# Half of the modulation-vector chunks beside the delta rule go to TensorE

## The chip, the core and the metric

The kernel runs on one core of a Trainium2 chip. The metric is the device time of one execution in microseconds. Three executions of the kernel before took 2535.95, 2541.6 and 2545.97 us, so the median is 2541.6 us. The engines are named as in the profile: PE is the matrix engine, PEld its weight loads, DVE the vector engine, ACT the scalar engine, POOL the GpSimd engine, SP the engine that issues most DMAs.

## What is computed

The reference is a two-layer trunk over 256 latent tokens of width 2048, in float32. Cut to what matters:

```python
for layer in range(2):
    mx = split(silu(c) @ w_ada[layer] + b_ada[layer], 6)       # six modulation vectors of 2048
    h_x = rms_norm(x, g_pre_mix) * (1 + mx[1]) + mx[0]
    if layer == 0:   # attention heads, and a bidirectional gated delta rule, side by side
        y_x = attention_deltanet_mixer(h_x, h_c, ...)          # h_c: the context, modulated alike
    else:
        y_x = fourier_mix(h_x) @ w_fourier
    x = x + mx[2] * rms_norm(y_x, g_post_mix)
    f_x = swiglu(rms_norm(x, g_pre_ffn) * (1 + mx[4]) + mx[3], w_gate, w_up, w_down)
    x = x + mx[5] * rms_norm(f_x, g_post_ffn)
```

The change concerns the product `silu(c) @ w_ada`. Each modulation vector is a matrix of 2048 x 2048 against one vector.

## The kernel before

The first two modulation vectors of layer 0 are made at the start (`ada_half`, lines 359 to 383), where each 128 x 1024 piece of the matrix goes to DVE, to GpSimd or to PE by a letter in the string `WHO`. A piece on PE is eight matmuls of one 128 x 128 block each against a column of `c2c`, the silu of the vector as columns, into one PSUM tile, and one ACT copy out of it.

The other ten vectors are background work. They are cut into 160 chunks of 128 output elements, 16 to a vector, and each chunk into two halves, so 320 units. A unit (`ada_units`, line 277) loads a 128 x 1024 piece of 512 KB into one of the two buffers named `araw` (line 285) and multiplies and sums it on DVE against the vector spread over all partitions (`cb`), in one instruction with an accumulator (`ada_dot`, line 274). `bg(n)` (line 298) runs n units. `every(us)` sets a pace: `step()`, which is called between the matmuls of the projections, runs one unit each time that `clock` has moved on by that many microseconds. `clock` is no time of the chip: `mm` (line 132) adds to it, for each matmul, its columns over 2400, times four for plain float32 operands, with at least 64 columns counted. `ada_until(m)` runs what is missing of the first m vectors.

The weights of all projections come through `load_w1` (line 183): a 512 KB load into one of three buffers named `raw` (in some stretches two loads of five take `araw`), ACT rounds each half of it to fp32r (`whi`, line 197), and DVE or POOL subtracts to get the rest (`wlo`, line 203). Each product takes three fp32r matmuls.

Beside the delta rule the pace is 4.3 and all `wlo` are POOL's. The delta rule of the four groups of heads is written as generators (`gdn_a`, `gdn_b`, `fin_k` and others) that `step()` advances between the matmuls of the remaining projections. The order on each engine is set when the program is built, by a list scheduler that may move an instruction ahead of the place where it was written when its inputs and its buffer are free; each engine then runs its list strictly in order. In the two feed-forward parts the order of DVE is the written one.

Two masks of triangles (`k_tri`, 128 x 2 x 128) are read twice: at the start, and again at line 490 for the running sums of the gates, each time into one of three buffers named `K1` by a DMA on POOL's queue.

## Time and profile before

| | us |
|---|---|
| three executions, median | 2541.6 |
| the profiled execution, as timed | 2532.5 |
| its span, first to last instruction | 2530.7 |
| PE busy in the span | 2361.0 |
| DVE busy | 1836.5 |
| ACT busy | 1304.6 |
| POOL busy | 423.4 |

The profile is of one execution. Busy time of an engine is the time in which one of its instructions was running; for PE the end of a matmul is modelled, and matmuls overlap. Stages in the trace: up to 191 us the first two modulation vectors with the first projection; from 191 to about 720 us the delta rule, attention and their projections; to about 806 us the output projection; then the feed-forward part of layer 0 to about 1590, the Fourier mix to about 1790, and the feed-forward part of layer 1. A row of waits counts the idle time of an engine before an instruction by what ended it.

### The profile page before, as it was taken

How to read it: one execution, taken by the hardware profiler on the slowest of the kernel's cores; microseconds unless marked ns; L12 is line 12 of the kernel's file. 1: busy time of each engine (PE TensorE's matmuls, PEld its weight loads, DVE VectorE, ACT ScalarE, POOL GpSimd, SP SyncE). 2: the span in 40 equal slices, each digit the busy share in tenths (PEclk: the TensorE clock that was granted, in tenths of full speed). 3: DMA queues.
4: the chain of work that ended last, by engine and by line, in shares of the span. 5: the costliest groups of instructions: out<-in, count | busy, mean ns of one | idle time of the engine just before them, and what ended most of it. 6: DMA issues, size and time to landing. Idle time of an engine off the chain costs nothing.

```text
span 2530.7 us, 39215 instructions
## 1 busy us (share of the span) xinstructions
PE 2361.0 (93%) x14232; PEld 1992.5 (79%) x14232; DVE 1836.5 (73%) x3232; ACT 1304.6 (52%) x2385; POOL 423.4 (17%) x331
## 2 busy tenths in 40 slices
PE   5888978888899999999999999899999999999997
PEld 5877868877677788888888887697788888888886
DVE  7998778778757677877778778847666665555556
ACT  4446533535375655454445554746654554445455
POOL 4873523335531100000000000101100000000001
PEclk8889989989999999999999999999999999999998
DMA  7665778678846668989998988626577777666665
GB/s 274 229 234 179 241 217 261 232 231 263 278 158 210 207 212 316 315 314 312 320 318 308 319 312 316 237 95 214 192 236 242 229 240 233 192 191 186 194 202 199
DMA packets 218530, 611.14 MB, mean 241 GB/s; under 512 B 68920, under 2 KB 69928, under 8 KB 217568
## 3 DMA queue, kind: packets, MB, share of 16 engines
q1 hardware_dynamic: 168016, 581.59, 68.6%
q10 hardware_dynamic: 46528, 15.21, 2.7%
q0 software_dynamic: 3792, 11.85, 1.4%
q8 instruction: 111, 1.82, 0.3%
q14 instruction: 83, 0.68, 0.1%
HBM read 595.16 MB, written 13.40 MB: 240 GB/s over the span
## 4 chain that ended last, share of the span: by engine, by line
PE 71%; DVE 12%; DMA 7%; issue 4%; ACT 2%; POOL 2%; SPq 0%; ACTq 0%; DVEq 0%; POOLq 0%
PE acc L132 65%; PE sm L132 5%; DMA araw<-in_ada_d 4%; DVE araw L274 3%; DVE E L274 1%; DVE wlo L203 1%; POOL C L359 1%; DMA T<-dy 1%; PE sm L1237 1%; DVE C L514 1%; DVE T L730 1%; DMA T<-dz 1%; DMA S<-in_ctx 1%; DVE S L1154 1%; ACT whi L197 1%
## 5 line engine op out<-in xcount | busy, mean ns | idle before, releaser
L197 ACT ACTIVATE whi<-raw 128x512 fp32r<-128x512 f32 (+1 forms) x1306 | 817.7, 630 | 858.2 <-DVE wlo L203 457.3
L203 DVE TENSOR_TENSOR wlo<-raw,whi 128x512 fp32r<-128x512 f32 x1140 | 796.6, 707 | 442.9 <-ACT whi L197 440.4
L132 PE MATMUL acc<-whi,S 128*128 128x512 f32 x3312 | 1043.0, 393 | 3.9 <-ACT whi L197 2.2
L132 PEld LDWEIGHTS acc<-whi,S 128*128 128x128 f32 x3312 | 624.7, 189 | 134.3 <-ACT whi L197 3.1
L132 PE MATMUL acc<-wlo,S 128*128 128x512 f32 x1656 | 649.0, 392 | 2.9 <-POOL wlo L203 1.7
L274 DVE SCALAR_TENSOR_TENSOR araw<-araw,cb 128x1024 f32<-128x1024 f32 x320 | 411.9, 1288 | 67.0 <-DMA araw<-in_ada_d 66.3
L132 PEld LDWEIGHTS acc<-wlo,S 128*128 128x128 f32 x1656 | 312.9, 189 | 67.6 <-POOL wlo L203 2.7
L203 POOL TENSOR_TENSOR wlo<-raw,whi 128x512 fp32r<-128x512 f32 x166 | 240.6, 1462 | 431.5 <-ACT whi L197 416.2
L132 PE MATMUL acc<-S,whi 128*128 128x256 f32 x1152 | 246.4, 306 | 22.5 <-ACT whi L197 9.4
L132 PEld LDWEIGHTS acc<-S,whi 128*128 128x128 f32 x1152 | 201.6, 209 | 25.3 <-ACT whi L197 10.5
L1114 POOL DMA_DIRECT2D drow<-K x4 | 2.0, 508 | 1274.8 <-DVE K L1112 1274.8
L132 PE MATMUL acc<-S,wlo 128*128 128x256 f32 x576 | 173.8, 303 | 9.9 <-DVE wlo L203 6.8
L132 PEld LDWEIGHTS acc<-S,wlo 128*128 128x128 f32 x576 | 121.0, 210 | 12.5 <-DVE wlo L203 8.7
L132 PE MATMUL acc<-whi,ZT 128*128 128x512 f32 x384 | 122.5, 393 | 0.0
L132 PE MATMUL acc<-whi,KCH 128*128 128x512 f32 x320 | 110.9, 403 | 1.1 <-ACT whi L197 1.1
L132 PE MATMUL acc<-whi,A 128*128 128x512 f32 x312 | 106.0, 395 | 0.0
L132 PE MATMUL acc<-whi,T 128*128 128x512 f32 x296 | 99.7, 393 | 0.0
L132 PEld LDWEIGHTS acc<-whi,ZT 128*128 128x128 f32 x384 | 72.1, 188 | 15.5
L132 PE MATMUL acc<-wlo,KCH 128*128 128x512 f32 x192 | 77.8, 405 | 4.3 <-DVE wlo L203 4.1
L132 PE MATMUL acc<-wlo,ZT 128*128 128x512 f32 x192 | 74.8, 390 | 0.0
L132 PEld LDWEIGHTS acc<-whi,KCH 128*128 128x128 f32 x320 | 62.2, 194 | 15.3 <-ACT whi L197 1.5
L132 PE MATMUL acc<-wlo,T 128*128 128x512 f32 x176 | 68.6, 390 | 0.0
(447 smaller groups left out, 2945.1 us busy)
## 6 DMA issues: line engine op xcount, KB each, us to landing
raw<-in_w_gu SPq DMA_DIRECT2D x347, 512.0 KB, 4.4
araw<-in_ada_d SPq DMA_DIRECT2D x320, 512.0 KB, 4.7
raw<-in_w_dn SPq DMA_DIRECT2D x179, 512.0 KB, 4.4
raw<-in_w_att SPq DMA_DIRECT2D x40, 512.0 KB, 4.5
raw<-in_w_gdn SPq DMA_DIRECT2D x34, 512.0 KB, 4.4
raw<-in_w_out SPq DMA_DIRECT2D x30, 512.0 KB, 3.5
ZT<-in_ada_s SPq DMA_DIRECT2D x24, 512.0 KB, 3.6
raw<-in_w_four SPq DMA_DIRECT2D x21, 512.0 KB, 3.5
```

What stands on the lines that cost most here:

```text
L132: nc.tensor.matmul(out, l, r, start=start, stop=stop)
L197: S.activation(hi[:, :w], raw[:, c:c + w], AF.Copy)
L203: eng.tensor_sub(lo[:, :w], raw[:, c:c + w], hi[:, :w].bitcast(F32))
L274: V.scalar_tensor_tensor(out=junk, in0=w, scalar=1.0, in1=rows, op0=ALU.mult, op1=ALU.mult, accum_out=dst)
L359: nc.gpsimd.tensor_tensor(out=pr, in0=raw[:, ql], in1=ccb[h][:, ql], op=ALU.mult)
L514: V.scalar_tensor_tensor(out=ca[:, :, lo:hi], in0=pv[:, :, lo + o:hi + o], scalar=wconv[:, blk, j:j + 1], in1=ca[:, :, lo:hi], op0=ALU.mul ...
L730: V.tensor_tensor(out=tv, in0=Zi[:, 0:k, k:k + 1].to_broadcast([P, k, 16 - k]), in1=Y[:, k:k + 1, k:16].to_broadcast([P, k, 16 - k]), op=A ...
L1114: nc.gpsimd.dma_start(drow.rearrange("h k p -> (h k) p"), gt)
L1154: V.scalar_tensor_tensor(out=x[:, t, sl], in0=y[:, t, sl], scalar=r, in1=x[:, t, sl], op0=ALU.mult, op1=ALU.add)
L1237: nc.tensor.transpose(p[:, i * P:(i + 1) * P], hv[t][:, i * P:(i + 1) * P], ident)
```

## The change

`NPE = 60` and `by_pe(n)`: of the first 60 chunks each odd one, so 30 chunks or 60 units, all in the first four background vectors, is computed on PE as eight matmuls against `c2c` and an ACT copy of one column into the accumulator tile. The host lays those pieces out as 128 x 128 blocks that PE can take as stationary operands. The load of a unit is a function of its own, `ada_load(i)`, and `bg` calls it for the unit it is about to run and for the one after; `ada_until` leaves out the last one ahead. `raw` has four buffers in place of three. `k_tri` gets a buffer of its own and is read once. The region of on-chip memory that holds descriptors of DMAs from GpSimd is set to 8192 bytes per partition.

```diff
--- before.py
+++ after.py
@@ -63,9 +63,15 @@
 XE = 3
 RING0 = 'oAakzrraoz'
 RING = 'rozza'
+NPE = 60
 SK_EV = 2
 SK_M = 1
 SK_P = 2
+
+
+def by_pe(n):
+
+    return n < NPE and n % 2 == 1
 
 
 @with_exitstack
@@ -183,7 +189,7 @@
     def load_w1(src, n=1024, keep=()):
 
         nload[0] += 1
-        raw = T([P, 1024], "araw", 2) if pace[1] and not pace[0] and nload[0] % 5 > 2 else T([P, 1024], "raw", 3)
+        raw = T([P, 1024], "araw", 2) if pace[1] and not pace[0] and nload[0] % 5 > 2 else T([P, 1024], "raw", 4)
         nc.sync.dma_start(raw[:, :n], src)
         out = []
         for c in range(0, n, 512):
@@ -217,7 +223,7 @@
     nc.gpsimd.memset(ones, 1.0)
     epsc = C([P, 1], "epsc")
     nc.gpsimd.memset(epsc, EPS)
-    tri = T([P, 2, P], "K1", 3)
+    tri = C([P, 2, P], "tri")
     nc.gpsimd.dma_start(tri, a["k_tri"])
 
     maskd = []
@@ -274,33 +280,48 @@
         V.scalar_tensor_tensor(out=junk, in0=w, scalar=1.0, in1=rows, op0=ALU.mult,
                                op1=ALU.mult, accum_out=dst)
 
+    plan = [(l, m, k, h) for l in range(2) for m in range(2 if l == 0 else 0, 6) for k in range(KC) for h in range(2)]
+    ada_raw = {}
+    ada_n = [0]
+
+    def ada_load(i):
+        if i < len(plan) and i not in ada_raw:
+            ada_raw[i] = T([P, 1024], "araw", 2)
+            nc.sync.dma_start(ada_raw[i], a["ada_d"][i // 2, i % 2])
+
     def ada_units():
-        n = 0
-        for l in range(2):
-            for m in range(2 if l == 0 else 0, 6):
+
+        for i, (l, m, k, h) in enumerate(plan):
+            ada_load(i)
+            raw = ada_raw.pop(i)
+            if k == h == 0:
                 ac = T([P, KC, 2], "adaacc", 2)
-                for k in range(KC):
-                    for h in range(2):
-                        raw = T([P, 1024], "araw", 2)
-                        nc.sync.dma_start(raw, a["ada_d"][n, h])
-                        ada_dot(raw, cb[:, h], ac[:, k, h:h + 1], raw)
-                        if k == KC - 1 and h == 1:
-                            V.tensor_reduce(out=mc[:, l, m], in_=ac, op=ALU.add, axis=AX.X)
-                            V.tensor_tensor(out=mc[:, l, m], in0=mc[:, l, m], in1=bada[:, l, m], op=ALU.add)
-                        yield
-                    n += 1
+            if not by_pe(i // 2):
+                ada_dot(raw, cb[:, h], ac[:, k, h:h + 1], raw)
+            else:
+                p = sm()
+                for kk in range(8):
+                    mm(p[:, 0:1], raw[:, kk * P:(kk + 1) * P], c2c[:, h * 8 + kk, 0:1], kk == 0, kk == 7)
+                S.activation(ac[:, k, h:h + 1], p[:, 0:1], AF.Copy)
+            if k == KC - 1 and h == 1:
+                V.tensor_reduce(out=mc[:, l, m], in_=ac, op=ALU.add, axis=AX.X)
+                V.tensor_tensor(out=mc[:, l, m], in0=mc[:, l, m], in1=bada[:, l, m], op=ALU.add)
+            yield
 
     ada_it = ada_units()
-    ada_n = [0]
-
-    def bg(n):
-        for _ in range(n):
-            if ada_n[0] < 320:
+
+    def bg(n, more=True):
+
+        for q in range(n):
+            if ada_n[0] < len(plan):
+                ada_load(ada_n[0])
+                if more or q < n - 1:
+                    ada_load(ada_n[0] + 1)
                 next(ada_it)
                 ada_n[0] += 1
 
     def ada_until(mods):
-        bg(max(0, 32 * mods - ada_n[0]))
+        bg(max(0, 32 * mods - ada_n[0]), False)
 
     def rstd(ssq, n, dim):
         r = col(n)
@@ -339,7 +360,7 @@
     def ada_half(i):
 
         k, m, h = i // 4, i // 2 % 2, i % 2
-        tag, n = {"a": ("araw", 2), "o": ("OG", 2), "z": ("ZT", 4), "r": ("raw", 3), "k": ("KCH", 2), "4": ("T4", 2), "A": ("A", 2)}[RING0[nraw[0]] if nraw[0] < len(RING0) else RING[nraw[0] % len(RING)]]
+        tag, n = {"a": ("araw", 2), "o": ("OG", 2), "z": ("ZT", 4), "r": ("raw", 4), "k": ("KCH", 2), "4": ("T4", 2), "A": ("A", 2)}[RING0[nraw[0]] if nraw[0] < len(RING0) else RING[nraw[0] % len(RING)]]
         nraw[0] += 1
         raw = T([P, 1024], tag, n)
         nc.sync.dma_start(raw, a["ada_s"][i])
@@ -487,8 +508,6 @@
     lbmg = C([P, 4, 8, 2], "lbmg")
     egc = C([P, 4, 8, 2], "egc")
     egl = C([P, 4, 8, 2], "egl")
-    tri = T([P, 2, P], "K1", 3)
-    nc.gpsimd.dma_start(tri, a["k_tri"])
     pgc = sm()
     for d in range(2):
         gd = T([P, 32], "gd", 2)
@@ -1468,7 +1487,9 @@
     for l in range(2):
         for m in range(2 if l == 0 else 0, 6):
             for k in range(KC):
-                dl.append(wa[l, :, m, k, :].T.reshape(P, 2, 1024).transpose(1, 0, 2))
+                w = wa[l, :, m, k, :]
+                dl.append(w.reshape(2, 8, P, P).transpose(0, 2, 1, 3).reshape(2, P, 1024) if by_pe(len(dl))
+                          else w.T.reshape(P, 2, 1024).transpose(1, 0, 2))
     o["ada_d"] = c(np.stack(dl, 0))
     w = g["w_in"][0]
     gd = w[:, 1536:4608].reshape(2, 8, P, 24, P)
@@ -1507,7 +1528,7 @@
     from concourse.bass_utils import run_bass_kernel_spmd as _run
 
     arrays = prep({n: inputs[n] for n in _INS})
-    nc = _bacc.Bacc("TRN2", target_bir_lowering=False, num_devices=1)
+    nc = _bacc.Bacc("TRN2", target_bir_lowering=False, num_devices=1, dynamic_dma_scratch_size=8192)
     a = {}
     for n, v in arrays.items():
         a[n] = nc.dram_tensor(f"in_{n}", v.shape, mybir.dt.from_np(v.dtype), kind="ExternalInput").ap()
```

## Rows read from the trace of the kernel before

**Rows 1.** The page: busy tenths of PE in 40 slices, its granted clock below.

```profile
PE   5888978888899999999999999899999999999997
PEclk8889989989999999999999999999999999999998
```

**Rows 2.** Windows: length, busy us of PE, PEld, DVE, ACT, POOL, clock, DMA share, GB/s.

```profile
191.00:720.00 529.00, 447.85 (x5070) 397.15 (x5071) 420.28 (x890) 254.34 (x509) 220.72 (x167) 0.93 0.77 238
...
900.00:1100.00 200.00, 200.00 (x899) 165.76 (x899) 154.69 (x252) 100.36 (x162) 0.00 (x0) 1.00 0.85 295
```

**Rows 3.** PE's waits from 191 to 720: waiting <- ender: us, times, longest.

```profile
PE sm L132 <- issue: 18.4, 6, 4.8
PE sm L132 <- DVE St L884: 9.4, 4, 3.2
PE sm L132 <- DVE rowhl L142: 9.1, 2, 8.8
PE sm L132 <- DMA T<-dy: 7.9, 2, 6.5
PE acc L132 <- POOL wlo L203: 4.8, 4, 1.9
```

**Rows 4.** Group of DVE, 191 to 720: count, busy us, mean ns, idle before, ender.

```profile
L274 DVE SCALAR_TENSOR_TENSOR araw<-araw,cb 128x1024 f32<-128x1024 f32 x128 | 177.9, 1393 | 67.0 <-DMA araw<-in_ada_d 66.3
```

**Rows 5.** Timeline near 451: start, us, instruction, [idle before <-ender].

```profile
451.09 1.23 DVE L274 SCALAR_TENSOR_TENSOR araw<-araw,cb 128x1024 f32<-128x1024 f32 x1 [2.48 <-DMA araw<-in_ada_d]
...
452.24 0.69 DVE L767 COPY E<-sm 128x512 f32<-128x512 f32 x1
...
452.98 1.25 PE L132 MATMUL sm<-E,T 32*32 32x32 f32 x126 [2.05 <-DVE E L767]
```

**Rows 6.** The chain that ended last, 191 to 720, by line.

```profile
by line: DMA araw<-in_ada_d 20.8%; DVE araw L274 13.0%; issue 10.9%; PE acc L132 10.7%; PE sm L132 6.1%; DMA T<-dy 3.8%; DVE C L514 3.3%; DVE T L730 2.9%; DMA T<-dz 2.8%; DVE T L732 2.4%; DVE K L709 1.9%; POOL wlo L203 1.5%; DMA dz<-Zc 1.2%
```

**Rows 7.** Timeline: PE pieces of the first stage, and a one-column matmul group.

```profile
105.67 1.84 PE L132 MATMUL sm<-c2c,araw 128*128 128x2 f32 x16
107.37 0.36 PE L132 MATMUL sm<-S,whi 128*128 128x256 f32 x1
...
146.77 3.41 PE L132 MATMUL sm<-c2c,raw 128*128 128x2 f32 x16
150.04 0.78 PE L132 MATMUL acc<-S,whi 128*128 128x256 f32 x2
...
252.91 0.95 PE L132 MATMUL sm<-ones,K 128*128 128x1 f32 x8
```

**Rows 8.** Timeline: a burst of small matmuls, and steps of 256-column ones.

```profile
440.06 0.40 PE L132 MATMUL acc<-S,whi 128*128 128x256 f32 x2
...
440.42 0.40 PE L132 MATMUL acc<-S,whi 128*128 128x256 f32 x2
...
446.10 1.40 PE L132 MATMUL sm<-T,Zc 32*32 32x32 f32 x128
```

**Rows 9.** Timeline near 441: a dot's end frees its buffer, the next load.

```profile
441.38 0.08 DVE L274 DVE_READ_ACCUMULATOR araw<-araw,cb 128x1 f32 x1
...
441.48 0.33 SPq L285 DMA_DIRECT2D araw<-in_ada_d  x1
```

**Rows 10.** DMA issues of the page: count, KB, median us to landing.

```profile
araw<-in_ada_d SPq DMA_DIRECT2D x320, 512.0 KB, 4.7
```

**Rows 11.** Line L350, the copy after a PE piece; its ACT's idle time before.

```profile
L350 ACT ACTIVATE K<-sm x14: 147/173/174, 56.5 to 191.5; 128x2 f32<-128x2 f32 x14
...
  PE sm L132: 21.4, 8
```

**Rows 12.** ACT's waits from 191 to 720.

```profile
ACT whi L197 <- PE acc L132: 85.3, 39, 7.2
```

**Rows 13.** Timeline of POOL near 223.

```profile
223.63 0.58 POOL L491 DMA_DIRECT2D K<-in_k_tri  x1 [12.99 <-DVE K L457]
```

**Rows 14.** Tile araw: weight loads that take its buffers; durations ns, first and last start.

```profile
L187 SPq DMA_DIRECT2D araw<-in_w_four x16: 327/328/383, 1617.6 to 1753.7; - x16
```

## The prediction, made before the changed kernel was run

> **What bounds the kernel now.** I read the page's slices first. PE is at nine tenths or more in most slices and lower in the first quarter [rows 1]. The windows then split the span. In a feed-forward stretch PE is busy 200.00 of 200 us at full clock with DVE at 155, so nothing taken from DVE there is worth anything. From 191 to 720 us, 529 us beside the delta rule, PE is busy 447.85 us and idle 81, the granted clock is 0.93, and DVE is busy 420.28 [rows 2]. That stretch is the only one in which the change moves work: the 60 units belong to the first four background vectors, and 128 units run in it [rows 4].
>
> In that stretch I looked at the dots: 177.9 us at 1.393 each, with 67.0 us of DVE idle before them, nearly all ended by the landing of their own load [rows 4]. DVE is thus occupied 420 + 67 = 487 of 529 us, 92%. The timeline shows what this does to PE: a dot waits 2.48 us for its load, a copy queued behind it runs at 452.24, and PE, idle for 2.05 us, goes on at 452.98 [rows 5]. The chain agrees: loads of units 20.8% and dots 13.0% of the stretch, PE's own lines below 17% [rows 6]. So DVE's queue is what PE waits for, and the change attacks the right queue. The question is the price on PE.
>
> **PE pieces, the large term.** A piece of the same kind in the first stage is 16 passes (each float32 matmul shows two) from 105.67 until the next matmul at 107.37: 1.70 us at full clock, and 3.27 us, 146.77 to 150.04, in a stretch at the lower level of 1.2 GHz [rows 7]. A one-column group there costs about the same per pass, 8 in 0.95 us [rows 7]. So 60 x 1.70 = **102 us** are added to PE inside a stretch in which it has 81 idle. What can pay for it:
>
> *Idle time.* Of the 81 us, 18.4 are ended by "issue", which I leave. The two longest rows of DVE are 9.4 and 9.1; a landing ended 7.9 and POOL's `wlo` 4.8 [rows 3]. DVE loses 60 x 1.47 = 88 us of dots (1.39, and 0.08 for the accumulator [rows 4, 9]). The pace counts 8 x 64 x 4 / 2400 = 0.85 us for each piece, 0.43 a unit on average, so by the program's own count of its matmuls the stretch, which was written with 114 units at 4.3, gets 114 x 4.3 / 3.87 = 127, about 12 more: 18 us of dots come back. DVE's occupation falls to about 487 - 88 + 18 - 33 = 384 us, if half of its waits for loads go with half of the dots. I take the DVE-ended waits as nearly gone, and half of the others as covered by pieces that happen to lie ahead of them: 44 of the remaining 63 us. The bounds are 20 and 63.
>
> *Overlap of matmuls.* Busy PE is not full PE: two 256-column matmuls that span 0.40 us are followed three steps later, after 0.36 us, by the next two [rows 8], so one that ends a burst counts some 0.15 us with nothing behind it. Over the 60 or so waits that is some 10 us; I take 8, with bounds 4 and 11.
>
> *Clock.* A mean of 0.93 of two levels means 14% of 529, so 74 us, at the lower one; PE is busy 85% of the time, so at most 31 us are lost to it. Denser PE should keep the clock up, but the bursts of 128 matmuls of 32 columns [rows 8] and the "issue" waits stay. I take 20; bounds 8 and 31.
>
> *Waits for loads, now on PE.* PE works its list in order, so a piece whose load has not landed stops all matmuls behind it. At the dots' rate, 67.0 / 128 = 0.52 us [rows 4], that is 31 us for 60; the pieces of the first stage, with more buffers, had no idle time before them, so 0 is the other end. I take 6, since PE will come to its pieces late.
>
> **The load begun a piece ahead** I cost at nothing. A load already goes out as its buffer is freed: the accumulator read begins at 441.38 and takes 0.08, and SP issues at 441.48 [rows 9], which is the pattern of the stretch. Two buffers and 4.7 us of landing [rows 10] set the rate, and neither changes. Outside the stretch it can cost: `ada_until` spares the one ahead, but a unit run by the pace leaves a loaded buffer behind, and the strips that share `araw` for weights [rows 14] then have one of the two left, against one more of `raw`. I take 0; bounds -5 and +10.
>
> **Fourth raw buffer.** In the stretch ACT waits 85.3 us for PE to free `whi` [rows 12], so weights stand ready before PE wants them: 0. **Triangles.** The second read stood on POOL's queue for 12.99 us behind a DVE result [rows 13], with `wlo` behind it; PE's waits for `wlo` are 4.8 us in all, and they are inside the idle time above. **ACT copies**: 60 x 0.17 us, and idle before them of 21.4 us in 8 of 14 cases [rows 11], so up to 92 us if each waits for its piece; ACT is busy 254 of 529 [rows 2]. What is queued behind on ACT, `whi` and the exponentials, would wait up to a piece's length, 1.7 us; `whi` is ahead of PE. I take 0, with some 10 us in the range. **The later stretches** lose 12 dots where DVE has room, and **the smaller descriptor region** serves POOL's few DMAs: 0 for both.
>
> **Sum.** 102 - 44 - 8 - 20 + 6 = **+36 us**. The profiled execution took 2532.5 us (span 2530.7 and 1.8 around it), so the changed one should show about 2568; the median of the runs shown, 2541.6, stands 9 above the profiled one, and the prediction is made for it: 2541.6 + 36 = **2578**.
>
> **Rivals.** *Absorbed.* PE's room is larger than its idle time says, and the pieces fit: 102 - 60 - 11 - 31 = 0, so **2542**. For it: DVE at 92% is what PE waits for. Against: it wants every payer at its bound. The Trainium skill (Perfetto Trace Analysis, "Identifying the Most-Contended Engine") judges PE by the busy share of its weight loads and not by matmul busy time; by that the stretch has 529 - 397 = 132 us of room [rows 2], and 102 fit. The feed-forward stretch shows 166 of 200 at full PE [rows 2], so the trace puts the end of that measure at 83%, not 100%.
>
> *DVE alone was the bound.* If all waits of PE but the "issue" ones came from DVE's queue, pieces sat only where PE would wait, the clock stayed up, and the earlier triangles and the fourth buffer freed the "issue" waits too, the payers sum to 81 + 11 + 31 = 123 and the time is 2541.6 - 21 = **2521**. It decides for faster from 115 us on (102 and the 13 of half a per cent), 94% of all that is there. A stretch at such density exists only where no delta rule runs.
>
> *The piece costs less.* If weight loads of a piece hide under matmuls of other work, a pass could cost as little as one of the 32-column burst, 1.40 / 128 = 0.011 us [rows 8]: 60 x 16 x 0.011 = 11 in place of 102, and **2487**. Against it: every group in the trace runs its passes in a row at 0.106 [rows 7]. The Trainium skill (TensorE: Matmul & The Clock Gate, "Back-to-back issue gap") gives about 60 cycles, 25 ns, to a matmul of 1 to 64 columns; by that the pieces are an estimated 24 us and the sum is -42. The trace disagrees for passes in a row, at 106 ns each [rows 7].
>
> *Coupled queues.* Dots and pieces share two buffers in turn, so PE waits for a load that waits for a dot that waits for PE: loads at 31, idle time bought only 20, clock 8: 102 - 20 - 4 - 8 + 31 = +101, **2643**.
>
> **How the numbers follow.** About half a per cent, 13 us, is what a measurement of this kernel can tell from no change. Forecast, slower by 13 to 80: 0.60. Absorbed, within 13: 0.20. DVE alone: 0.11. Cheaper piece: 0.04. Coupled: 0.05. So faster 0.15, same 0.20, slower 0.65. The range leaves out the cheap piece, the coupled queues and the outer part of the faster case: 2526 to 2622.
>
> **What would show it.** PE pieces at 1.6 to 1.9 us in groups of 16 passes; PE busy from 191 to the output projection about 100 us up, its idle time near 35, the clock at 0.95 or more; DVE's idle time before dots about half; waits of PE named by loads of units near 6 us; no change from 900 us on. I am wrong if the delta rule's stretch ends no later than 720 us, or if PE's idle time there stays above 70.

## The result, and the profile after

The changed kernel took 2675.73 us (median of 4 runs, 2671.36 to 2678.53); the kernel before, on the same chip, 2538.77. The ratio is 1.0541, with a 95% interval of 1.0514 to 1.0567. The forecast was slower, 2578, and that sign held; the loss of 137 us is almost four times the 36 forecast, and the time lies above the range of 2526 to 2622. The profiled execution has a span of 2669.5 us, 138.8 more than before.

The page first: PE's busy tenths, its granted clock, and the two groups of PE that are new, with count, busy us, mean ns of one, idle time before and its ender.

```profile
PE   5889999998999889999999999889899999999998
...
PEclk8889979898999999999999999889899999999999
...
L138 PEld LDWEIGHTS sm<-c2c,araw 128*128 128x128 f32 x1008 | 127.7, 203 | 5.8 <-issue 2.5
...
L138 PE MATMUL sm<-c2c,araw 128*128 128x1 f32 (+1 forms) x1008 | 124.3, 253 | 1.9 <-DMA araw<-in_ada_d 1.1
```

The slices of the delta rule are now mostly nines, so PE is seldom idle there, yet the stretch became longer. 960 of these 1008 passes are the 60 pieces, and PE sat idle for 1.9 us in all before them.

Windows (length, busy us of PE, PEld, DVE, ACT, POOL, clock, DMA share, GB/s), over the delta rule and the output projection, two parts of it, and a part of the first feed-forward stage:

```profile
191.00:860.00 669.00, 621.55 (x6399) 561.04 (x6399) 353.46 (x850) 305.70 (x665) 217.49 (x181) 0.92 0.61 191
300.00:400.00 100.00, 95.26 (x1095) 83.68 (x1094) 46.33 (x127) 30.22 (x73) 29.37 (x27) 0.86 0.64 180
600.00:720.00 120.00, 105.42 (x1128) 89.05 (x1129) 63.33 (x158) 45.95 (x106) 45.49 (x39) 0.87 0.63 193
1000.00:1200.00 200.00, 200.00 (x899) 165.73 (x898) 154.67 (x252) 102.00 (x166) 0.00 (x0) 1.00 0.86 294
```

The same stretch of the kernel before, which ends earlier there:

```profile
191.00:770.00 579.00, 495.88 (x5409) 434.88 (x5410) 444.43 (x971) 291.91 (x598) 236.36 (x181) 0.94 0.73 226
```

DVE fell from 77% busy to 53% and PE rose from 86% to 93%. The clock did not rise with it: 0.94 before, 0.92 after, and 0.86 in parts of it. The feed-forward window is what it was.

The chain that ended last, by line, in the same stretch:

```profile
by line: PE sm L138 29.7%; PE acc L138 29.0%; issue 9.5%; DMA araw<-in_ada_d 2.6%; POOL wlo L209 2.5%; DVE T L751 2.1%; DVE araw L280 1.7%; DMA T<-dz 1.7%; DVE C L533 1.5%; DMA dz<-Zc 1.5%; DMA T<-dy 1.1%; DMA dy<-T 1.1%; PE sm L1040 1.1%; 
```

Loads and dots, a third of the chain before [rows 6], are 4% of it, and PE's own lines 59%. The change moved the chain onto PE.

Waits, of PE, DVE, ACT and SP in that stretch (waiting <- ender: us, times, longest):

```profile
PE sm L138 <- issue: 13.4, 5, 3.8
PE acc L138 <- ACT whi L203: 6.0, 4, 3.4
...
PE sm L138 <- DMA araw<-in_ada_d: 1.1, 1, 1.1
...
DVE araw L280 <- DMA araw<-in_ada_d: 52.5, 25, 6.0
...
ACT adaacc L305 <- PE sm L138: 101.2, 48, 5.6
...
SPq L290 <- PE sm L138: 213.4, 53, 14.0
SPq L193 <- POOL wlo L209: 175.4, 50, 13.5
SPq L290 <- DVE araw L280: 93.6, 30, 6.2
```

PE waited 1.1 us for loads of units. A unit's load waits for a buffer, now mostly until a piece is done on PE (213.4 us).

Two neighbouring pieces in the timeline (start, us, instruction, idle before):

```profile
371.05 1.92 PE L138 MATMUL sm<-c2c,araw 128*128 128x1 f32 x16 [1.11 <-DMA araw<-in_ada_d]
...
372.83 0.36 PE L138 MATMUL acc<-S,whi 128*128 128x256 f32 x1
...
374.71 3.41 PE L138 MATMUL sm<-c2c,araw 128*128 128x1 f32 x16
...
378.16 0.17 ACT L305 ACTIVATE adaacc<-sm 128x1 f32<-128x1 f32 x1 [4.98 <-PE sm L138]
```

The first takes 1.78 us to the next matmul, the second 3.4 us, as the two pieces of [rows 7] did. The windows of the two pieces show the two levels, 1.00 and 0.50:

```profile
371.05:372.80 1.75, 1.75 (x16) 1.75 (x16) 0.00 (x0) 0.00 (x0) 0.00 (x0) 1.00 1.11 278
374.71:378.10 3.39, 3.39 (x23) 3.38 (x26) 0.69 (x1) 0.00 (x0) 0.00 (x0) 0.50 0.74 269
```

To see which stage grew I took the start of the same matmuls into the projections' accumulators in each trace: those of number 2300, 2800, 5600 and 6400, counted from 0, which begin at 775, 913, 1560 and 1819 us in the kernel before. The first stage reaches from 191 us to number 2300, near the end of the output projection. The other columns are named by the stage that fills most of them; "to FFN" ends at number 2800, some 100 us into the feed-forward part. In the first stage I sorted the steps from one PE instruction to the next: the step that its shape takes at full clock is "work", what a step of the lower clock takes longer is "half-rate", the rest is "stall". "Half-rate" is thus time lost at the lower of the two clock levels. Working rows for all kernels of this document, in us:

```
                     first stage = work + half-rate + stall | to FFN | FFN 0 | Fourier | FFN 1
before                  584.4      428.6    23.7    132.0   | 138.1  | 646.7 | 259.2 | 711.4
after                   675.5      536.2    41.2     98.1   | 148.8  | 646.8 | 298.6 | 708.8
e1  no load ahead       677.7                               | 138.3  | 646.8 | 262.1 | 711.4
e2  no pieces           580.8      429.7    24.0    127.0   | 143.0  | 646.7 | 296.6 | 711.0
e3  128-column passes   674.3      538.4    22.6    113.2   | 139.3  | 646.8 | 299.2 | 711.1
e4  30 pieces           634.0      478.6    41.4    113.8   | 155.5  |       | 295.7 |
e5  half pieces         619.1      483.7    31.8    103.5   | 144.3  |       | 295.9 |
e6  only loaded         614.4      431.8    32.8    149.7   | 134.9  |       | 296.3 |
e7  rest alone          576.5      430.0    22.0    124.4   | 138.3  | 646.8 | 260.9 | 710.0
e8  three araw          671.0      531.9    41.3     97.8   | 139.5  |       | 259.2 |
e9  copy on DVE         681.4                               | 141.6  |        | 297.8 |
e10 not counted         645.0      523.8    34.8     86.2   | 148.1  |       | 299.0 |
e11 short dots          578.5      428.0    21.7    128.7   | 137.1  |       | 298.6 |
e12 e6, not counted     573.7                               | 134.6  |       | 296.3 |
e13 e6, slower pace     583.4                               | 136.7  |       | 305.5 |
e14 e7, slower pace     568.8                               | 135.8  |       | 305.8 |
e15 after, slower pace  656.1                               | 157.3  |       | 297.9 |
e16 e14, FFN pace       570.0      429.5    23.7    116.7   | 135.6  | 649.4 | 260.2 | 710.6
e17 e1 and e10          655.7      524.2    44.0     87.5   | 142.4  | 646.8 | 261.9 | 710.2
```

The changed kernel lost 91 us in the first stage (work +107.6, half-rate +17.5, stalls -33.9), 11 between numbers 2300 and 2800, and 39 in the Fourier mix, long after the last piece. Those are two losses at two places, and the forecast had only the first.

The second one shows in the issues of weight loads for the strips, on SP, in the changed kernel:

```profile
1693.26 0.33 SPq L193 DMA_DIRECT2D araw<-in_w_dn  x1
1693.64 3.69 SPq L193 DMA_DIRECT2D raw<-in_w_dn  x3
1701.29 6.32 SPq L193 DMA_DIRECT2D araw<-in_w_dn  x2
1709.03 5.21 SPq L193 DMA_DIRECT2D raw<-in_w_dn  x3
1715.06 7.41 SPq L193 DMA_DIRECT2D araw<-in_w_dn  x2
```

and in e7, which has no load ahead:

```profile
1579.53 0.33 SPq L193 DMA_DIRECT2D araw<-in_w_dn  x1
1581.39 0.33 SPq L193 DMA_DIRECT2D raw<-in_w_dn  x1
1583.74 0.33 SPq L193 DMA_DIRECT2D araw<-in_w_dn  x1
1584.12 1.74 SPq L193 DMA_DIRECT2D raw<-in_w_dn  x2
1590.83 1.49 SPq L193 DMA_DIRECT2D araw<-in_w_dn  x2
1592.37 2.87 SPq L193 DMA_DIRECT2D raw<-in_w_dn  x3
```

Two loads of five take `araw`. In e7 a pair goes out within 1.49 us; in the changed kernel the second waits some 6 us for the first, because only one buffer is left: the other holds the unit that the last paced step loaded ahead. That unit's load went out at 1689.12, and the dot that reads it runs at 1955.83, behind the strips:

```profile
1689.12 0.33 SPq L290 DMA_DIRECT2D araw<-in_ada_d  x1
...
1955.83 1.22 DVE L280 SCALAR_TENSOR_TENSOR araw<-araw,cb 128x1024 f32<-128x1024 f32 x1
```

### The profile page after: what moved, and what is told of

Same layout as the page of the kernel before. It is cut to its first block, busy times and chain, and to the rows that moved or that the text cites. A ratio compares the mean times of both kernels' runs of the same rounds, so it can differ in the third digit from the quotient of the medians.

```text
span 2669.5 us, 41138 instructions
## 1 busy us (share of the span) xinstructions
PE 2502.9 (94%) x15192; PEld 2125.1 (80%) x15192; DVE 1745.5 (65%) x3112; ACT 1315.4 (49%) x2447; POOL 408.7 (15%) x330
## 4 chain that ended last, share of the span: by engine, by line
PE 74%; DVE 8%; DMA 6%; issue 5%; ACT 3%; POOL 3%; ACTq 0%; SPq 0%; DVEq 0%; POOLq 0%
PE acc L138 62%; PE sm L138 10%; DVE wlo L209 2%; DMA araw<-in_w_four 2%; POOL C L380 2%; ACT whi L203 1%; DVE E L280 1%; DMA araw<-in_ada_d 1%; DVE araw L280 1%; PE sm L1256 1%; POOL wlo L209 1%; DVE S L1173 1%; DMA S<-in_ctx 1%; DVE T L751 1%; POOL S L445 1%
## 5 line engine op out<-in xcount | busy, mean ns | idle before, releaser
L280 DVE SCALAR_TENSOR_TENSOR araw<-araw,cb 128x1024 f32<-128x1024 f32 x260 | 323.5, 1244 | 74.1 <-DMA araw<-in_ada_d 57.1
L209 POOL TENSOR_TENSOR wlo<-raw,whi 128x512 fp32r<-128x512 f32 x166 | 227.3, 1378 | 549.0 <-ACT whi L203 536.3
L138 PEld LDWEIGHTS sm<-c2c,araw 128*128 128x128 f32 x1008 | 127.7, 203 | 5.8 <-issue 2.5
L138 PE MATMUL sm<-c2c,araw 128*128 128x1 f32 (+1 forms) x1008 | 124.3, 253 | 1.9 <-DMA araw<-in_ada_d 1.1
```

What stands on the lines that cost most here:

```text
L138: nc.tensor.matmul(out, l, r, start=start, stop=stop)
L209: eng.tensor_sub(lo[:, :w], raw[:, c:c + w], hi[:, :w].bitcast(F32))
L280: V.scalar_tensor_tensor(out=junk, in0=w, scalar=1.0, in1=rows, op0=ALU.mult, op1=ALU.mult, accum_out=dst)
```

## The experiments

Diffs are against the changed kernel. Unless a run says otherwise, the ratio is to the kernel before on the same chip, with its 95% interval.

**What the load ahead costs.** e1 leaves it out.

```diff
-                if more or q < n - 1:
-                    ada_load(ada_n[0] + 1)
```

> The changed kernel without the load of the unit after the one being run; all else stays. Theory A: the unit loaded ahead by the pace keeps one of the two araw buffers through the strips in which weights use them too, and that is the loss after 860 us (by the time of equal matmuls 11 us up to the feed-forward part and 39 us from 1662 to 1960); so the time falls by about 50, to 2626 (2615 to 2640), the two junctions are as long as before the change, and the delta rule's stretch stays within 10 us. Rival B: that loss comes from the fourth raw buffer or the smaller descriptor region, and the time stays at 2676 (within 10). Rival C: the load ahead pays beside the delta rule, then that stretch gets longer by over 10 us.

Measured 2626.03, ratio 1.0341 (1.0325 to 1.0356): 50 us less. All of it lies behind the first stage, which stayed at 677.7. The load ahead brought the delta rule nothing and cost 50 us later.

e8 keeps the load ahead and gives `araw` three buffers and `raw` three.

```diff
-            ada_raw[i] = T([P, 1024], "araw", 2)
+            ada_raw[i] = T([P, 1024], "araw", 3)      # and so in load_w1; "raw", 4 -> 3
```

> The changed kernel with three araw and three raw buffers in place of two and four. Theory A: beside the delta rule the passes are the price and the buffers are not, so that stretch stays within 12 us; after it two araw buffers are left for the weights, one being held, so the later loss of 49 us shrinks to 10 or less: 2630 (2618 to 2642). Rival B: pieces and dots in two shared buffers tie the queues; a third one loosens that and the stretch gets shorter by 30 or more: below 2605. Rival C: the later loss is not the held buffer but the order of the loads: the time stays above 2660.

Measured 2632.29, ratio 1.0363: the Fourier part is back at 259.2, the first stage moved by 4.5 us only. So the late loss is the held buffer, and the early loss is not a lack of `araw` buffers, as far as a third one (with one `raw` less) can show.

**What the pieces cost.** e2 has none; all units are dots.

```diff
-NPE = 60
+NPE = 0
```

> The changed kernel with no chunk on TensorE (NPE 0): all 320 units are dots on DVE, the load ahead, the resident triangles and the fourth raw buffer stay. Theory A: the 91 us that the delta rule's stretch gained (107 of pieces and 17 of clock, less 34 of waits) are the pieces' own, so the time falls to about 2585 (2575 to 2597) with the two later losses, some 50 us, still there. Rival B: the stretch is longer since the load ahead ties the two buffers, pieces or not: then it stays above 2640.

Measured 2570.30, ratio 1.0122 (1.0107 to 1.0137), 5 us below the range of theory A: the first stage is 580.8, and the pieces cost 95 us there. What remains above the kernel before, 31 us by the ratio, is the held buffer less what the other parts bring (e7 below): 40 us between e2 and e7.

e4 makes every fourth chunk a piece.

```diff
-    return n < NPE and n % 2 == 1
+    return n < NPE and n % 4 == 1
```

> The changed kernel with every fourth chunk of the first 60 on TensorE in place of every second: 30 pieces and not 60. Theory A: PE's time is what a piece costs wherever it lies, 1.8 us less what waits give back: half of 91 is gained, 2676 to about 2631 (2620 to 2640). Rival B: the first pieces fall into PE's idle time and only the later ones cost: then 30 cost nearly nothing and the time is near 2590. Rival C: pieces cost by tying the two engines' queues through two buffers; with dots three times as many as pieces the tie stays, and the time stays above 2650.

Measured 2635.39, ratio 1.0378. Half of the pieces, with half of their count, cost 53 of the 95 us in the first stage: there is no free first half that fits into PE's idle time.

e5 has all pieces with four of their eight blocks, and counts them in full in the program's clock.

```diff
-                for kk in range(8):
-                    mm(p[:, 0:1], ...)
+                for kk in range(4):
+                    mm(p[:, 0:1], ...)
+                clock[0] += 4 * 64 * 4 / 2400.0
```

> The changed kernel with four of the eight blocks in each piece, so 8 passes and not 16 on TensorE; the other half of those sums is left out. Loads, copies, counts of the pace and the load ahead stay. Theory A: what a piece costs is the time of its passes, 16 x 0.112 us; half of them cost half, so 60 x 0.9 = 54 us come back and the time is about 2622 (2612 to 2634). Rival B: a piece costs by tying the two queues through two buffers; its length matters little and the time stays above 2650.

Measured 2604.44, ratio 1.026: 71 us less than the changed kernel. In the first stage it is 56 us (675.5 to 619.1) for 54 us of passes left out: the price goes by PE's time in passes. Theory A took the cost from the passes alone and had 2612 at the least. Of the other 15 us the later stages show 5 in the traces; the rest is the distance of the two profiled executions from their medians (e5's was its slowest, the changed kernel's its fastest).

**Waits of ACT.** e9 takes the result off PSUM on DVE.

```diff
-                S.activation(ac[:, k, h:h + 1], p[:, 0:1], AF.Copy)
+                V.tensor_copy(ac[:, k, h:h + 1], p[:, 0:1])
```

> The changed kernel with the one-column copy out of each piece done by VectorE in place of ScalarE. In the changed kernel ScalarE is idle for 101.2 us before 48 of the 60 copies, waiting for the piece, and near 378 us its queue issues the delta rule's next DMA only after such a copy (a wait of 4.98 us). Theory A: a piece costs its passes on TensorE and no more; the stretch stays within 12 us and the time is 2664 to 2688. Rival B: a good part of the 95 us is ScalarE held by the copies, with the delta rule's DMAs and exponentials behind; VectorE, with room now, holds up less: the time falls by 25 or more, below 2650.

Measured 2676.14, ratio 1.0549. ACT's 101.2 us of waiting went to DVE, in the waits of that kernel:

```profile
DVE adaacc L305 <- PE sm L138: 114.5, 48, 9.1
```

and the time did not move. It makes no difference which of the two engines waits for a piece; that the wait costs nothing on either is likely by that, but not shown.

**The clock.** e3 gives PE the same passes with 128 columns in place of one.

```diff
-                    mm(p[:, 0:1], raw[...], c2c[:, h * 8 + kk, 0:1], kk == 0, kk == 7)
+                    nc.tensor.matmul(p[:, 0:P], raw[...], c2c[:, h * 8 + kk, 0:1].to_broadcast([P, P]), ...)
+                    clock[0] += 64 * 4 / 2400.0
```

> The changed kernel with the column of c2c spread to 128 columns as the moving operand of each piece: the same number of weight loads and matmuls, and the same sums in each of the 128 columns, of which the first is copied out. Float32 matmuls of 128 columns step at 0.11 us in the trace before, as those of one column do, so a piece should still take about 1.8 us. Theory A: one-column passes leave the clock at its lower level more often (0.86 to 0.91 in the two worst stretches); with 128 columns the granted clock beside the delta rule goes back to 0.94 or more and the time falls by about 17, to 2659 (2648 to 2666). Rival B: the clock falls because of the waits and of the bursts of 32-column matmuls around them; then the clock stays and the time is 2676 within 8.

Measured 2659.86, ratio 1.0472. Windows of e3, and its piece passes by shape:

```profile
191.00:860.00 669.00, 604.50 (x6413) 545.41 (x6412) 363.08 (x857) 305.85 (x665) 219.55 (x181) 0.95 0.62 193
300.00:400.00 100.00, 90.15 (x1122) 79.66 (x1121) 51.15 (x143) 31.09 (x79) 32.09 (x32) 0.93 0.68 185
L304 PE MATMUL sm<-c2c,araw 128*128 128x128 f32 x960 | 121.9, 281 | 7.1 <-DMA araw<-in_ada_d 5.4 <-DVE araw L280 1.1 <-ACT adaacc L306 0.4
```

A pass of 128 columns costs no more than one of a single column, and the clock rose from 0.92 to 0.95 (from 0.86 to 0.93 between 300 and 400). The total fits the theory that the clock pays, but the stages say otherwise: the half-rate excess fell by 18.6 and the stalls rose by 15.1, and the first stage stayed (675.5 and 674.3). The two traces differ by 8 us only, with 9.5 in the column "to FFN" (148.8 to 139.3); e3's profiled execution was its slowest and the changed kernel's its fastest, so the other 8 us of the 16 can't be placed, and up to that much may belong to the first stage. The lower clock goes with the one-column passes; it is at most a small part of what the first stage is long for.

**What freeing DVE is worth.** e11 keeps the 60 units on DVE but sums 8 of 1024 elements.

```diff
-                p = sm()
-                for kk in range(8): ...
-                S.activation(...)
+                ada_dot(raw[:, 0:8], cb[:, h, 0:8], ac[:, k, h:h + 1], raw[:, 0:8])
```

> The changed kernel with the 60 units as dots on VectorE again, but over 8 of the 1024 elements, so that each takes a fraction of its 1.39 us; the rest of those sums is left out. Loads, buffers, order of consumers and pace are those of the kernel with all dots (2570 us). It shows what 60 dots' time on VectorE is worth. Theory A: VectorE's time is not what the stretch waits for: 2560 to 2575. Rival B, the forecast's: its queue is what TensorE waits for, some 80 us less of work brings 30 us or more: 2540 or less.

Measured 2561.71, ratio 1.0098. Windows of e2 and of e11:

```profile
191.00:770.00 579.00, 501.83 (x5438) 439.62 (x5438) 453.47 (x979) 291.18 (x602) 243.30 (x182) 0.94 0.72 226
```

```profile
191.00:760.00 569.00, 492.13 (x5408) 432.68 (x5409) 377.14 (x972) 288.70 (x594) 223.75 (x180) 0.95 0.72 228
```

DVE is busy 76 us less, and the first stage is 2.3 us shorter; the whole time is 6 us shorter by the ratios, 9 by the medians. Where the freed time went is in DVE's longest wait, of e2 and of e11:

```profile
DVE araw L280 <- DMA araw<-in_ada_d: 58.1, 41, 6.4
```

```profile
DVE araw L280 <- DMA araw<-in_ada_d: 91.4, 62, 5.7
```

33 us of it became more waiting for loads. PE's stalls stayed, 127.0 and 128.7. DVE's time for dots did not set this stage.

**What the program's own count costs.** e6 loads the 60 units, takes one column of each through ACT, and counts the passes that it doesn't run.

```diff
-                p = sm()
-                for kk in range(8): ...
-                S.activation(ac[:, k, h:h + 1], p[:, 0:1], AF.Copy)
+                clock[0] += 8 * 64 * 4 / 2400.0
+                S.activation(ac[:, k, h:h + 1], raw[:, 0:1], AF.Copy)
```

> The changed kernel in which the 60 units are loaded and then used by nobody but a copy of one column on ScalarE: neither TensorE nor VectorE has their work, which is left out. It shows what taking 60 dots from VectorE is worth alone, beside 2570 for the kernel in which all units are dots. Theory A: it is worth little, some 15 us (the sum of waits and half-rate time fell only from 156 to 139 us with the pieces), so the time is 2550 to 2572. Rival B, the forecast's: VectorE's queue is what the stretch waits for, worth some 50 us and more: 2525 or less.

Measured 2595.96, ratio 1.0222. Neither theory had that: with less work than e2 it is 26 us slower than e2. Its first stage holds 142 loads of units against 130 in e2, since the count of passes moves the pace on.

e12 is e6 without the count; e13 is e6 at a pace of 4.73, by which the stage holds 131 loads.

```diff
-                clock[0] += 8 * 64 * 4 / 2400.0     # e12
-MRATE = 4.3
+MRATE = 4.73                                        # e13, from e6
```

> The kernel in which the 60 units are only loaded and one column of each is copied by ScalarE (their work is left out), now without the count on the program's own clock. With the count it took 2596 us. Theory A: what made it slower than the kernel with all dots (2570) is ScalarE, which waits in order for loads (52 us in 23 waits): the time stays at 2596 within 10. Rival B: it is the count, which draws the delta rule's steps together: 2572 or less.

> The kernel with the 60 units only loaded and one column of each copied by ScalarE (their work is left out), with the count, and with the pace of that stretch at 4.73 in place of 4.3, so that as many units are written into it as before the change (114). With the count at 4.3 it took 2596 us, uncounted 2561. Theory A: the count costs because it brings 12 more units, each some 3 us of the stretch by its turn in the two shared buffers: 2548 to 2568. Rival B: it costs because the delta rule's steps stand closer in projection matmuls, which the pace does not change: 2586 to 2606.

Measured 2561.47 (e12, ratio 1.0103) and 2569.19 (e13, ratio 1.0118). e12 is as rival B had it, e13 is 1 us above the range of theory A. In the first stage the count costs 41 us (614.4 to 573.7), of which the slower pace takes back 31 (583.4). So 11 units more in this stage (142 loads against 131) cost some 31 us. The 10 that are left may come from where the count puts the rest, since the same clock also says when the delta rule's generators take their steps; no run has that alone.

e10 and e15 ask the same of the changed kernel: pieces not counted, and pieces counted at the pace of 4.73.

```diff
-                    mm(p[:, 0:1], raw[...], ..., kk == 0, kk == 7)
+                    nc.tensor.matmul(p[:, 0:1], raw[...], ..., start=kk == 0, stop=kk == 7)   # e10
-MRATE = 4.3
+MRATE = 4.73                                                                                   # e15
```

> The changed kernel in which the matmuls of pieces do not advance the program's own clock, so that the pace brings as many units into the stretch as before the change and the delta rule's steps stand as far apart in projection matmuls as before. Theory A: the count hardly matters beside 1.8 us of real time a piece: within 15 us of 2676. Rival B: the count draws the steps of the delta rule together and leaves their waits bare (the run without any work for the 60 units was 33 us longer in that stretch than the one with dots): the time falls by 25 or more, below 2650.

> The changed kernel with the pace of the delta rule's stretch at 4.73 in place of 4.3, which takes back the 12 units that the pieces' count brings; 60 pieces, load ahead and all else stay. Uncounted pieces took 2646. Theory A: those 30 us are the 12 units': 2636 to 2656. Rival B: they are the steps drawn together: 2666 to 2686.

Measured 2646.41 (e10, ratio 1.0433) and 2661.3 (e15, ratio 1.0484). So the count costs 29 us of the whole time, as rival B of e10 had it, and the pace alone takes back 14, between the two theories of e15. In the first stage it is 30 (675.5 to 645.0) and 19 (656.1), but these stages hold less work: in both runs 4 of the 60 pieces ran behind matmul number 2300, some 7 us of passes, and the loads of units ahead of it are 115 in e10 and 116 in e15. There are 128 in the changed kernel, 129 in the kernel before and 130 in e2. So the changed kernel ran no more units in this stage than the kernel before; with the count left out it runs fewer.

e17 leaves out the load ahead and the count together.

> The changed kernel with two of its losses off at once: no load ahead, and the pieces' matmuls not counted in the program's clock. Theory A (the 50 us of the held buffer and the 30 us of the counting are separate places and add up, and what is left is the pieces' own passes, about 70): 2596, 2585 to 2606. Theory B (the two overlap, since both act through the same two buffers): 2610 to 2626.

Measured 2600.06, ratio 1.0243 (1.0216 to 1.0271). By single runs 2675.7 - 49.7 - 29.3 = 2596.7: the two losses add up, as theory A had it, and what is left, some 62 us over the kernel before, is the passes less what the other parts bring.

**What is left without the pieces.** e7 has no pieces and no load ahead; the triangles, the fourth buffer and the smaller region remain.

```diff
-NPE = 60
+NPE = 0
-                if more or q < n - 1:
-                    ada_load(ada_n[0] + 1)
```

> The changed kernel with neither the pieces nor the load ahead: what is left is the resident triangles, the fourth raw buffer and the smaller descriptor region. Theory A: the two losses add up and are all of the loss; the junctions are as before the change and the delta rule's stretch 3 to 4 us shorter: 2531 (2525 to 2537), a little under the kernel before. Rival B: the fourth buffer and the triangles are worth nothing: 2539 within 3.

Measured 2530.15 against 2539.39, ratio 0.9965 (0.9951 to 0.998): 9 us faster than before, 8 of them in the first stage. Which of the three parts brings it was not tried.

e14 is e7 at a pace of 5.2, with 109 units in the first stage in place of 129.

> The kernel with neither pieces nor load ahead (2530 us; resident triangles, four raw buffers), with the pace of the delta rule's stretch at 5.2 in place of 4.3: some 19 units fewer there, done in the feed-forward part of layer 0, where VectorE has room. Theory A: each unit in the stretch costs it 2.5 to 3.4 us by its turn in the two buffers: 47 to 65 us less, 2465 to 2485. Rival B: it was not the number of units: 2530 within 8.

Measured 2560.02, ratio 1.009; neither theory had that. Twenty units fewer made the first stage 7.7 us shorter, 0.4 us a unit, and a wait of PE in the Fourier mix appeared:

```profile
PE acc L138 <- ACT ZT L203: 42.3, 1, 42.3
```

The units that were not run had to be caught up by `ada_until` in front of the third strip (18 loads from 1716 us on). e16 runs them in the feed-forward part.

```diff
-MRATE = 4.3
+MRATE = 5.2
-F0RATE = 3.9
+F0RATE = 3.5
```

> The kernel without pieces and without the load ahead, at the slower pace of 5.2 beside the delta rule, and with the first feed-forward part's pace at 3.5 in place of 3.9, so that some 18 more units run there. Theory A (what the slower pace lost was one catch-up ahead of the third Fourier strip, and the feed-forward stretch has room on DVE for 18 more dots of 1.4 us): the 42 us wait for ZT is gone, and the kernel lands 8 us under the 2530 of the same kernel at the old paces, at 2522, 2512 to 2528. Theory B (the feed-forward stretch has no room for more units, or the fewer units beside the delta rule bring nothing that lasts): 2530 to 2560.

Measured 2518.88 against 2537.47, ratio 0.9926 (0.9908 to 0.9944). The wait is gone (Fourier 260.2), the feed-forward part took the units for 2.6 us, as its window shows with DVE at 164 of 200 and PE still full:

```profile
900.00:1100.00 200.00, 200.00 (x899) 165.81 (x899) 164.47 (x273) 100.19 (x161) 0.00 (x0) 1.00 0.91 328
```

It beats both kernels, with units taken away from the delta rule to where DVE has room, and no piece on PE. By the ratios it is 19 us under the kernel before, 9 of which e7 has already.

## Why the prediction was right in sign and wrong in size

By the traces the loss is 138.8 us: 91 in the first stage, where the forecast had 36, and 48 behind it, where it had none. Two steps failed. Idle time, overlap and clock were to pay 72 of the pieces' 102 us and paid 16; and the load begun a piece ahead was put at nothing, where the buffer that it holds cost 50. The predicted row of terms was 102 - 44 - 8 - 20 + 6 + 0 = 36. By term:

- **Pieces, 102.** Measured 107.6 of work at full clock. Right. The step is 112 ns in the median, against 106 in [rows 7].
- **Idle time -44 and overlap -8.** Measured -34 of stalls for both together, 18 less than forecast but within the bounds, 24 to 74 in sum. But the reason given failed. I read DVE as 92% occupied by adding its waits for loads to its busy time, and its queue as what PE waits for. Those waits were slack: e11 takes 76 us of dots from DVE, gains 2.3 in the stage, and leaves PE's stalls where they were. The stalls fell where pieces ran, not where DVE was freed. Nor did these waits halve with half of the dots: 52.5 us are left of 66.3 [rows 4]. And the timeline's 2.48 and 2.05 us [rows 5] was one case that I took for the rule.
- **Clock -20.** Measured +17.5, outside its bounds of 8 and 31 and of the other sign. I had argued that a denser PE keeps the clock up. PE became denser, 93% busy, and the clock fell from 0.94 to 0.92; e3, the same passes with 128 columns, has 0.95. As e3's first stage is hardly shorter, this term is not a price that simply adds to the others: time won back there came out as stalls.
- **Waits of PE for loads, +6.** Measured 1.1. Right.
- **The load ahead, 0.** Measured 50 (e1, e8), against bounds of -5 and +10. This is the largest miss. The place and the mechanism stood in the prediction, a loaded buffer left behind while the strips share `araw`; I did not work out its price, and the fourth `raw` that was set against it did not make it up. What the price needs was there: behind the first feed-forward part 26 weight loads take `araw`, as the rows of the tile below count them, and with one buffer left they go one after another, 6 to 7 us for two, instead of in pairs.

```profile
L193 SPq DMA_DIRECT2D araw<-in_w_four x16: 327/328/328, 1741.3 to 1902.4; - x16
L193 SPq DMA_DIRECT2D araw<-in_w_dn x6: 327/328/328, 1693.3 to 1734.2; - x6
L193 SPq DMA_DIRECT2D araw<-in_w_gu x4: 327/328/328, 1910.0 to 1933.1; - x4
```

- **The count of the pieces, 18 us of DVE, 0 for PE.** Measured 29 in the whole time (e10), 14 of them by the pace (e15). I had 114 units grow to 127 in the stretch; the trace before had 129 there already, beyond the 114 written, and the changed one has 128, so no dots came back: DVE's busy time fell by 91 us (444.43 to 353.46), where I had 70. Without work for the 60 units, one unit more costs 2.8 us of the stage (e13); one of the last 20 below 130 costs 0.4 (e14). Why is not settled. The two buffers would be a reason, but a third one hardly moved the stage (e8).
- **ACT copies, fourth buffer, triangles, 0.** Nearly right: e9 shows that moving the copies' waits to DVE changes nothing, and e7 gives -9 us for the other two together with the smaller region.

Worked by runs, in whole time by the ratios: -9 for the rest (e7), +40 for the held buffer (e2 against e7), -5 for the relieved DVE (e12 against e2), +84 for the uncounted passes (e10 against e12) and +27 for their count make the 137 measured. They must, since each run is set against the one ahead of it; each step is known to some 4 to 12 us. Other runs test them: the held buffer costs 51 with the pieces there (e1), and sixty uncounted pieces in place of dots cost 71 (e17 against e7) or 79 (e10 against e2). The first stage alone does not part passes and count so well, since e10 holds fewer units and pieces there than e12 and the changed kernel.

Of the rivals, "coupled queues" came nearest in time, 2643, by a mechanism that did not occur: PE's waits for loads are 1.1 us. "Absorbed" rested on weight loads as the measure of PE's room. The Trainium skill (Perfetto Trace Analysis, "Identifying the Most-Contended Engine") takes PE's weight-load busy share, beside the share of peak operations, as that measure. Read up to 100% it left 132 us free in the stretch, and the 60 pieces cost 95 there all the same. Read up to the 83% of the full feed-forward stretch [rows 2], which the prediction named as its end, it left 42 (0.83 x 529 - 397), and after the change the stretch stands at 84% (561.04 of 669.00): so read, the trace agrees that there was not room for 102. "The piece costs less" was excluded by [rows 7], and e5 confirms it; the 25 ns a matmul that the Trainium skill (TensorE: Matmul & The Clock Gate, "Back-to-back issue gap") states for few columns is its floor for the matmul alone; the same section says that in a stream of weight loads and matmuls both set the spacing. Here each pass has a weight load of its own (1008 of each), and a pass takes 112 ns.

Where the general fault lies: PE had 81 us of idle time in 529, and I took more than half of it as room. Of the 107 us of passes the kernel got 28 to 36 back (79 and 71 uncounted), and e4 shows no free first part: 30 pieces, 54 us of passes, cost 53 with their count. Why the waits took so little stays open. That a piece of 1.8 us is too long for them is not shown: counted in the trace before, 19 of PE's 46 waits from 191 to 720 us are longer than 1.8 us, and they hold 62 of the 81.

## What to carry to other kernels

Idle time of PE beside a chain of dependent small steps is not by itself room for new work: take half of the new work first, and see whether that half is free. A wait for a load in an engine's queue need not be occupation of that engine; shorten its work in one run and see where the time goes. A buffer loaded ahead is paid for by whoever shares its ring, also stages later, and work that counts in a pace moves other work with it; count what a stage holds in both traces before a difference in it is given a cause.

## What the runs showed of the hardware

- A float32 pass with 128 stationary columns takes the same time with one moving column as with 128: 118.8 and 121.9 us busy in all for 960 passes, by the groups of the changed kernel and of e3, and 112 ns in the median from one pass to the next in both. (The 254 and 281 ns of a single pass have modelled ends.)

```profile
L138 PE MATMUL sm<-c2c,araw 128*128 128x1 f32 x960 | 118.8, 254 | 1.9 <-DMA araw<-in_ada_d 1.1 <-DVE A L719 0.8
```

- With such passes of one column the granted clock was lower, although PE was busier, than in e3, whose edit changes their columns alone: 0.86 of full speed between 300 and 400 us with PE busy 95.26 of 100 us, against 0.93 in e3 with 90.15. The two levels show within 4 us of one another, in the two pieces at 371.05 and 374.71.
- A feed-forward stretch with PE full at 200 of 200 us took 17 more dots on DVE (172 unit loads against 155 in e14) and the 512 KB of each, at 328 GB/s in the window shown, and the whole part became 2.6 us longer (e16).
